# A hybrid decoder layer on one core: compact rotation tables, b and c loaded a block ahead, and the state-space side transfers on another queue

## The chip, the cores and the metric

The kernel runs on 1 core of one Trainium2 chip. The metric is the device time of one execution in microseconds (us), lower is better. The kernel before was run three times: 1270.53, 1271.02 and 1276.63 us, median 1271.02.

## The reference, cut to what matters

One layer of a decoder, computed for a prompt (16 meta tokens and 512 new ones) and for 8 sample tokens; 536 columns in all, of width 2048.

```python
xn = rmsnorm(x, norm_gain)
q, k, v, z_a, u, z_s, g_a, g_s = split(xn @ w_in)          # 2048 x 8704
q, k = rope(rmsnorm(q)), rope(rmsnorm(k))
o_a = sink_attention(q, k, v)         # sliding window of 128, 16 meta keys, a sink
# S5 branch: 64 groups of 16 inputs, 64 complex states each
lam_bar = exp((a_re + i a_im) * dt)
b_bar = (lam_bar - 1) / lam * (b_re + i b_im)
h[t] = lam_bar * h[t-1] + b_bar @ u[t]                     # complex scan over time
y = gelu(real(c @ h) + d_skip * u)
y = y * sigmoid(y @ w_glu + b_glu)
out = x + (sigmoid(g_a) * (o_a * silu(z_a)) @ w_attn_out
         + sigmoid(g_s) * (y * silu(z_s)) @ w_ssm_out) @ w_out
```

The outputs are the new activations, the key and value windows, and the final states.

## The kernel before, in words

The matmuls carry the time. Every weight tile of 128 x 1024 is loaded in float32 (tile `raw`), cast by ScalarE to a reduced-precision high part (`whi`, L1014 or L1080), and VectorE forms the rest (`wlo`, L1015 or L1081). A unit of work, `mm` (L1174), multiplies a weight tile with the activations in 48 matmuls: for each of 8 k-slices high by high, high by low, low by high, two column halves of 260 or 268 each. A large middle part, `quad` (L1410), does the same with four blocks at once, by sums of blocks (L1079) that save products. TensorE runs this stream without a pause if the tiles are there.

Everything else runs as background work. Python generators in three lanes (class `Background`) are stepped between the matmuls: `bg.step` is called after every few k-slices, `yield cost` uses up a budget, and `yield None` ends the lane's turn until the next step. So a `yield None` moves what follows it one step later in TensorE's program. In attention a step is 4 k-slices, 24 matmuls. A scheduler then lays out each engine's queue in an order by its own estimate of times; on the chip each queue runs strictly in that order. Waiting instructions therefore hold up all that is queued behind them on the same engine, and for a DMA that means on the queue of the engine that issues it: SyncE (SP in the profile) for `nc.sync`, GpSimd (POOL) for `nc.gpsimd`.

The background work that the change touches, in order of time:

- `ssm_prep` (to about 400 us) computes the constants of the state-space branch. Its last part writes the rotation tables: for each of 8 blocks `ub`, four products (L308), a difference (L310) and a sum (L311) on VectorE make the table in one scratch tile `t[0]` of 128 x 528, and two DMAs (L314) write it to the DRAM tensor `tabD`, each row of 66 numbers twice, so that the real and the imaginary half of a head lie side by side. The scratch tile is the same for each block, so the products of the next block wait until both DMAs have read it.
- `ssm_consts` (about 450 to 710 us, one pass for each of 8 blocks) loads `f4` (4 DMAs, L347), `bN` (L349) and `c` (L351) into single buffers, scales `bN` and `c` on ScalarE (12 + 32 small instructions, `times`, L362), loads `B` (L381) and `tab` (L383, from `tabD`), forms the products of `B` with `f4` (L391 to L394), and makes the block's short convolution kernel: a matmul (L411), `k0` (L416, L417), a DMA to DRAM (`kD`, L419) and four DMAs back into the matrix `T` (L421). All these DMAs are on SP.
- `ssm_load` fetches the block's inputs `U` with 12 DMAs from POOL (L440 to L444), after `uD` was stored, on POOL too (L1620).
- `ssm_block` does the block: matmuls of `B` with `U` (L473), multiplication by the table (L487, L488), the sums (L493, L494), two scans with a carry (L507, L501 to L505), multiplication back (L513), the states `H` (L518, L519), matmuls of `T` with `U` (L529) and of `CL` with `H` (L532), the gelu (L539 to L546), and six DMAs on SP that store the result to `yD` (L551, L553).
- Attention starts when the last block is done. It loads the tables of the rotary embedding, the keys, values and queries (`sbw`, L703), rotates them, makes the query tiles `QT` (L795) and then takes the score matmuls (L811, L812). Between the first queries and the first scores it lets `NDELAY` = 3 steps pass. Its result is cast to the tile `A` (L1693), which the matmuls with `w_attn_out` read.

The weight loads of the main stream (`raw`, L1013) share SP with all of this.

Of the kernel before, what the change touches and what calls it, by code (L numbers as in the profile page):

```python
# [8 lines left out]
F32 = mybir.dt.float32  # L9
# [3 lines left out]
ALU = mybir.AluOpType  # L13
AX = mybir.AxisListType
P = 128
L = 66
NB = 2
NC = 132
# [3 lines left out]
def bc(ap, axis, n):  # L22

    a = ap.unsqueeze(axis)
    s = list(a.shape)
    s[axis] = n
    return a.to_broadcast(s)
# [122 lines left out]
def ssm_prep(nc, K, tmp, psum, dram, R, ident, a_prm, later, behind, room):  # L150

    v = OnPool(nc, tmp)
# [5 lines left out]
    t = tmp.tile([P, 32], F32, name="th")  # L158
# [11 lines left out]
    x = tmp.tile([P, 32], F32, name="xr")  # L170
# [8 lines left out]
    n = tmp.tile([P, 2, 32], F32, name="sc_n")  # L179
    k = tmp.tile([P, 2, 32], F32, name="sc_k")  # L180
    r = tmp.tile([P, 2, 32], F32, name="sc_r")
    s = tmp.tile([P, 2, 32], F32, name="sc_s")
    q = tmp.tile([P, 2, 32], F32, name="sc_q")
# [28 lines left out]
    g = tmp.tile([P, 2, 32], F32, name="f_g")  # L212
# [19 lines left out]
    r4 = K["r4"]  # L232
# [45 lines left out]
    c = tmp.tile([P, 2, 32], F32, name="zc")  # L278
# [4 lines left out]
    car = K["car"]  # L283
# [13 lines left out]
    FD = dram.tile([8, 32, P], F32, name="FD")  # L297
    nc.sync.dma_start(out=FD.rearrange("(h k) a s -> (k a) h s", h=2), in_=fts)
    R["FD"] = FD
    yield 0.0  # L300
    R["tabD"] = dram.tile([8, P, 16 * L], F32, name="tabD")
    t = [f.rearrange("p (r a i j) -> p r a i j", r=2, a=4, j=6) for f in (room[:, 0:8 * L], room[:, 8 * L:16 * L])]
    for ub in range(8):
        ps = slice(4 * ub, 4 * ub + 4)
        with behind():
            for r in range(2):
                for e in range(2):
                    v_.tensor_tensor(out=t[r][:, e], in0=bc(T11[:, e, ps], 3, 6), in1=bc(T6[:, r, ps], 2, 11), op=ALU.mult)  # L308
            a, b = (f.rearrange("p r a i j -> p r (a i j)") for f in t)
            v_.tensor_tensor(out=a[:, 0], in0=a[:, 0], in1=b[:, 1], op=ALU.subtract)  # L310
            v_.scalar_tensor_tensor(out=a[:, 1], in0=a[:, 1], scalar=-1.0, in1=b[:, 0], op0=ALU.mult, op1=ALU.subtract)  # L311
            d = R["tabD"][ub].rearrange("p (x r l) -> p x r l", r=2, l=L)
            for r in range(2):
                nc.sync.dma_start(out=d[:, :, r], in_=t[0].rearrange("p r a i j -> p (r a) (i j)"))  # L314
        yield 2.4


# [21 lines left out]
def ssm_consts(nc, pool, dram, R, D, ub, a_bT, a_bN, a_cT, e32, d_skip, later, free):  # L339

    v = nc.vector
    ps = slice(4 * ub, 4 * ub + 4)

    f4 = pool.tile([P, 2, 512], F32, name="f4", bufs=1)
    for j in range(4):
        row = R["FD"][3 - j::4, ps, :].rearrange("i a s -> i (a s)").unsqueeze(0).to_broadcast([32, 2, 512])
        nc.sync.dma_start(out=f4[32 * j:32 * j + 32], in_=row)  # L347
    bN = pool.tile([P, 4, 2, 32], F32, name="bN", bufs=1)
    nc.sync.dma_start(out=bN, in_=a_bN[:, ps])  # L349
    c = pool.tile([P, 4, 2, 32], F32, name="c", bufs=1)  # L350
    nc.sync.dma_start(out=c, in_=a_cT[:, ps])  # L351
    yield 0.0
    yield None

    t1 = pool.tile([P, 4, 2, 4, 32], F32, name="ct1", bufs=1)
    t2 = pool.tile([P, 4, 2, 4, 32], F32, name="ct2", bufs=1)
# [7 lines left out]
    for a in range(4):  # L364
        q = slice(4 * ub + a, 4 * ub + a + 1)
# [2 lines left out]
        times(s2[:, a], bN[:, a], R["nFim"][:, q])  # L368
    yield 0.0
    yield None  # L370
    for r, t in ((0, t1), (1, t2)):
        for k in range(4):
            for a in range(4):
                times(t[:, a, :, k], c[:, a], R["lamp"][:, r, k, 4 * ub + a:4 * ub + a + 1])
            if k % 2:
                yield 0.0
                yield None
    while not free():
        yield None
    B = pool.tile([P, 2, 512], F32, name="B")  # L380
    nc.sync.dma_start(out=B, in_=a_bT[ub])  # L381
    tab = pool.tile([P, 2, 4, 2, L], F32, name="tab")
    nc.sync.dma_start(out=tab.rearrange("p i a r l -> p (i a r l)"), in_=R["tabD"][ub])  # L383
    D["tab"] = tab
    CL = pool.tile([P, 4, 2, 5, 32], F32, name="CL")
    nc.scalar.copy(out=CL[:, :, :, 0], in_=c)
# [28 lines left out]
    k0 = pool.tile([P, P], F32, name="k0", bufs=1)  # L415
    nc.scalar.copy(out=k0[:, 32:P], in_=kp[:, 32:P])  # L416
    v.scalar_tensor_tensor(out=k0[:, 0:32], in0=e32, scalar=d_skip[:, ub:ub + 1], in1=kp[:, 0:32], op0=ALU.mult, op1=ALU.add)  # L417
    kD = dram.tile([P, P], F32, name="kD4", bufs=2)
    nc.sync.dma_start(out=kD, in_=k0)  # L419
    for j in range(4):  # L420
        nc.sync.dma_start(out=R["T"][ub % 2][32 * j:32 * j + 32, :, 32 * j:P], in_=kD.rearrange("(a q) x -> q a x", a=4)[:, :, 0:P - 32 * j])  # L421
    yield 0.3

    D["tab"] = tab
    d0 = R["d0"][ub % 2]
    d0v = d0.rearrange("p (a r) l -> p a r l", r=2)
    for i in range(2):
        nc.scalar.copy(out=d0v[:, :, i, 1:L], in_=bc(R["r4"][:, ps], 2, L - 1))
    D["d0"] = d0
    yield 0.0  # L430

# [15 lines left out]
def ssm_block(nc, pool, R, D, ub, y_out, later):  # L447
# [2 lines left out]

    v = nc.vector
    U, T = R["U"][ub % 2], R["T"][ub % 2]
    w = pool.tile([P, NB, 4, 2, L], F32, name="w", bufs=1)

    H = R["H"]
    ps = slice(4 * ub, 4 * ub + 4)
    nc.scalar.copy(out=H[:, :, :, 0:8], in_=R["N0"][:, ps])
    yield None
    tab = D["tab"]
# [17 lines left out]
    p1 = pool.tile([P, 2, 4, NB, L], F32, name="p1", tag="rt1", bufs=1)  # L477
    p2 = pool.tile([P, 2, 4, NB, L], F32, name="p2", tag="rt2", bufs=1)
    for h in range(2):
        for i in range(2):  # L480
            parts = [(slice(0, 2), bu[2 if h else i][:, 0:280].rearrange("p (e c) -> p e c", e=2))]
            if (h, i) == (1, 1):
                parts = [(slice(e, e + 1), place(1, 1, e).unsqueeze(1)) for e in range(2)]
            for es, b in parts:
                a = slice(2 * h + es.start, 2 * h + es.stop)
                bi = b[:, :, 0:NC].rearrange("p e (n l) -> p e n l", l=L)
                v.tensor_tensor(out=p1[:, i, a], in0=bi, in1=bc(tab[:, 0, a, 0], 2, NB), op=ALU.mult)  # L487
                v.tensor_tensor(out=p2[:, i, a], in0=bi, in1=bc(tab[:, 1, a, 0], 2, NB), op=ALU.mult)  # L488
                g = slice(4 * ub + a.start, 4 * ub + a.stop)
                v.tensor_tensor(out=R["sst"][:, g, i], in0=R["A0"][:, g, i], in1=b[:, :, NC:140], op=ALU.add)  # L490
        yield 2.2
    wv = w.rearrange("p n a r l -> p r a n l")
    v.tensor_tensor(out=wv[:, 0], in0=p1[:, 0], in1=p2[:, 1], op=ALU.subtract)  # L493
    v.tensor_tensor(out=wv[:, 1], in0=p1[:, 1], in1=p2[:, 0], op=ALU.add)  # L494
    yield 1.4
    for n in range(NB):
        if n:
            g = w[:, n - 1, :, :, L - 1]
            k1 = pool.tile([P, 4, 2], F32, name="k1", bufs=1)
            k2 = pool.tile([P, 4, 2], F32, name="k2", bufs=1)  # L500
            v.tensor_tensor(out=k1, in0=g, in1=bc(R["car"][:, 0, ps], 2, 2), op=ALU.mult)  # L501
            v.tensor_tensor(out=k2, in0=g, in1=bc(R["car"][:, 1, ps], 2, 2), op=ALU.mult)
            v.tensor_tensor(out=k1[:, :, 0], in0=k1[:, :, 0], in1=k2[:, :, 1], op=ALU.subtract)
            v.tensor_tensor(out=k1[:, :, 1], in0=k1[:, :, 1], in1=k2[:, :, 0], op=ALU.add)
            v.tensor_tensor(out=w[:, n, :, :, 0], in0=w[:, n, :, :, 0], in1=k1, op=ALU.add)  # L505
        wf = w[:, n].rearrange("p a r l -> p (a r l)")
        v.tensor_tensor_scan(out=wf, data0=D["d0"].rearrange("p a l -> p (a l)"), data1=wf, initial=0.0,  # L507
                             op0=ALU.mult, op1=ALU.add)
        yield 1.3 + 0.8 * n
    t1 = pool.tile([P, NB, 4, 2, L], F32, name="rt1", bufs=1)  # L510
    t2 = pool.tile([P, NB, 4, 2, L], F32, name="rt2", bufs=1)
    for t, i in ((t1, 0), (t2, 1)):
        v.tensor_tensor(out=t.rearrange("p n a r l -> p n (a r l)"), in0=w.rearrange("p n a r l -> p n (a r l)"),  # L513
                        in1=bc(tab[:, i].rearrange("p a r l -> p (a r l)"), 1, NB), op=ALU.mult)
    yield 2.5
    hv, v1, v2 = (t.rearrange(f"p {o} -> p r a n l", l=L) for t, o in
                  ((H[:, :, :, 9:9 + NC], "a r (n l)"), (t1, "n a r l"), (t2, "n a r l")))
    v.tensor_tensor(out=hv[:, 0], in0=v1[:, 0], in1=v2[:, 1], op=ALU.add)  # L518
    v.tensor_tensor(out=hv[:, 1], in0=v2[:, 0], in1=v1[:, 1], op=ALU.subtract)  # L519
    yield 1.4  # L520
# [4 lines left out]
    with later():  # L525
        for e in range(2):
            o = [bu[n][:, 140 * e:140 * e + 140] for n in range(2)]
# [8 lines left out]
    ga = pool.tile([P, 4, 140], F32, name="g", bufs=1)  # L536
    o = [(ga[:, n::2], bu[n][:, 0:280].rearrange("p (e c) -> p e c", e=2)) for n in range(2)]
# [9 lines left out]
    dst = y_out.rearrange("(a q) c -> q a c", a=4)  # L547
    for r in range(4):
        s, c = divmod(r, 2)
        o = 260 * c + 128 * s  # L550
        nc.sync.dma_start(out=dst[:, :, o:o + 128], in_=ga[32 * r:32 * r + 32, :, 12:8 + NC])  # L551
    for c in range(2):
        nc.sync.dma_start(out=dst[:, :, 260 * c + 256:260 * c + 260], in_=ga[0:32, :, 4 * c:4 * c + 4])  # L553
    yield 0.8


# [383 lines left out]
BUDGET2, BUDGET3, BUDGET4 = 6.0, 3.4, 4.8  # L940
HIGH = 4000
NLOAD = 3
NDELAY = 3
ATTC = (("kg", 1), ("kgs", 1), ("qg", 1), ("qgs", 1), ("mown", P), ("mprev", P), ("bd64", 4), ("sink", 16))
NXR = 10
NWARM = 9
# [1043 lines left out]
```

## Time and profile before

| | |
|---|---|
| median of 3 runs | 1271.02 us |
| the profiled execution | 1277.01 us, of it a span of 1275.2 us from the first to the last instruction |
| mean granted TensorE clock | 0.992 |
| TensorE matmul busy | 1254.0 us (98%), 10333 instructions |
| VectorE, ScalarE, GpSimd busy | 983.8, 632.1, 267.0 us |
| DMA | 226.75 MB, mean 178 GB/s |

In the profile PE is TensorE, DVE VectorE, ACT ScalarE. A row of a group or of the timeline names the line of the kernel, the engine, the operation, the tile written and the tiles read; brackets give the time that the engine sat idle before it and what ended that. The granted clock is 1.00 at full speed.

### The profile page before, as it was taken

The numbers are of one execution on the slowest core, as the hardware profiler recorded it, in microseconds if no ns is written. First come the engines' busy times: TensorE is split into PE (matmuls) and PEld (weight loads), VectorE is DVE, ScalarE is ACT, GpSimd is POOL, SyncE is SP. The second block draws the span as 40 slices with busy tenths as digits, with TensorE's granted clock in tenths as the row PEclk, the third lists the DMA queues.
The fourth block names the chain that finished last, engine by engine and source line by source line (L and its number), as shares of the span: only waits on it lengthen the run. The fifth ranks groups of instructions, "written<-read, shape, count | busy, mean of one in ns | idle before, by whom it ended". The sixth has DMA issues, their size and how long they took to land.

```text
span 1275.2 us, 26461 instructions
## 1 busy us (share of the span) xinstructions
PE 1254.0 (98%) x10333; PEld 1229.2 (96%) x10333; DVE 983.8 (77%) x1516; ACT 632.1 (50%) x1351; POOL 267.0 (21%) x437
## 2 busy tenths in 40 slices
PE   9999999999899999999999999999999999999998
PEld 9999999999889999999999998999999999999998
DVE  8686888888688755788879666979987467787775
ACT  8554444454344577555552243577665323354442
POOL 0003999930000014123232013120011000000000
PEclk9999999999899999989999998999999999999999
DMA  8544343344887475666665488677667665564441
GB/s 290 204 157 156 123 142 125 125 162 132 167 184 185 144 244 163 166 194 194 174 168 146 139 244 242 197 249 211 193 205 232 225 190 180 160 207 149 153 140 51
DMA packets 125728, 226.75 MB, mean 178 GB/s; under 512 B 38700, under 2 KB 64260, under 8 KB 125572
## 3 DMA queue, kind: packets, MB, share of 16 engines
q1 hardware_dynamic: 116964, 206.63, 53.0%
q0 software_dynamic: 8640, 18.45, 5.7%
q8 instruction: 81, 1.33, 0.4%
q14 instruction: 43, 0.35, 0.1%
HBM read 185.34 MB, written 40.59 MB: 177 GB/s over the span
## 4 chain that ended last, share of the span: by engine, by line
PE 81%; DMA 9%; DVE 5%; issue 2%; SPq 2%; ACT 1%; POOL 0%; DVEq 0%; POOLq 0%; ACTq 0%
PE mm L1174 39%; PE pr L1410 32%; DMA tabD<-work 3%; PE wg L860 2%; DMA sbw<-rawD 1%; PE aux L1410 1%; DMA xr<-in_x 1%; PE aux L1174 1%; DMA raw<-in_w 1%; DMA U<-uD 1%; PE aux L811 1%; PE aux L812 1%; DMA yD<-g 1%; PE mm L1731 1%; PE tr L842 1%
## 5 line engine op out<-in xcount | busy, mean ns | idle before, releaser
L1080 ACT CAST whi<-raw 128x1024 fp32r<-128x1024 f32 x168 | 173.2, 1049 | 186.0 <-DVE raw L1079 95.3
L1081 DVE TENSOR_TENSOR wlo<-raw,whi 128x1024 fp32r<-128x1024 f32 x168 | 206.8, 1252 | 57.8 <-ACT whi L1080 57.5
L1410 PE MATMUL pr<-tau,whi 128*128 128x260 f32 x992 | 182.0, 285 | 6.7 <-DVE z L1445 5.1
L1174 PE MATMUL mm<-xh,whi 128*128 128x260 f32 (+1 forms) x744 | 176.0, 289 | 1.4 <-DVE z L1211 0.8
L1014 ACT CAST whi<-raw 128x1024 fp32r<-128x1024 f32 (+3 forms) x124 | 118.2, 962 | 119.1 <-PE mm L1174 65.1
L1174 PE MATMUL mm<-xl,whi 128*128 128x260 f32 (+1 forms) x744 | 173.4, 286 | 0.0
L1174 PE MATMUL mm<-xh,wlo 128*128 128x260 f32 (+1 forms) x744 | 172.4, 286 | 0.0
L1015 DVE TENSOR_TENSOR wlo<-raw,whi 128x1024 fp32r<-128x1024 f32 (+3 forms) x124 | 137.6, 1118 | 37.2 <-ACT whi L1014 34.8
L1410 PEld LDWEIGHTS pr<-tau,whi 128*128 128x128 f32 x992 | 154.3, 190 | 7.1 <-DVE z L1445 5.3
L1410 PE MATMUL pr<-cb,whi 128*128 128x260 f32 x848 | 153.0, 283 | 0.0
L1410 PE MATMUL pr<-tau,wlo 128*128 128x260 f32 x496 | 140.6, 284 | 0.0
L1410 PEld LDWEIGHTS pr<-cb,whi 128*128 128x128 f32 x848 | 130.8, 189 | 0.2 <-ACT z L1444 0.2
L1174 PEld LDWEIGHTS mm<-xh,whi 128*128 128x128 f32 x744 | 124.7, 189 | 4.0 <-issue 2.2
L1174 PEld LDWEIGHTS mm<-xl,whi 128*128 128x128 f32 x744 | 124.9, 190 | 0.4 <-issue 0.4
L1174 PEld LDWEIGHTS mm<-xh,wlo 128*128 128x128 f32 x744 | 124.1, 189 | 0.0
L1079 DVE TENSOR_TENSOR raw<-raw 128x1024 f32<-128x1024 f32 x95 | 119.0, 1253 | 1.5
L1410 PE MATMUL pr<-cb,wlo 128*128 128x260 f32 x424 | 119.1, 283 | 0.2 <-DVE wlo L1081 0.2
L1410 PE MATMUL pr<-xl,whi 128*128 128x260 f32 x376 | 105.4, 283 | 0.0
L1174 PE MATMUL mm<-Y,whi 128*128 128x260 f32 x576 | 105.3, 286 | 0.0
L1410 PE MATMUL pr<-xh,wlo 128*128 128x260 f32 x376 | 104.9, 283 | 0.0
L1410 PE MATMUL pr<-xh,whi 128*128 128x260 f32 x376 | 104.7, 284 | 0.0
L1410 PEld LDWEIGHTS pr<-tau,wlo 128*128 128x128 f32 x496 | 94.1, 190 | 0.0
(426 smaller groups left out, 2974.0 us busy)
## 6 DMA issues: line engine op xcount, KB each, us to landing
raw<-in_w SPq DMA_DIRECT2D x202, 512.0 KB
gD<-z SPq DMA_DIRECT2D x36, 260.0 KB
t<-gD SPq DMA_DIRECT2D x32, 260.0 KB
cache<-in_vc POOLq DMA_DIRECT2D x16, 286.0 KB, 3.6
cache<-in_kc POOLq DMA_DIRECT2D x15, 288.0 KB, 3.6
xr<-in_x SPq DMA_DIRECT2D x16, 268.0 KB
xg<-in_x SPq DMA_DIRECT2D x8, 536.0 KB
tabD<-work SPq DMA_DIRECT2D x16, 264.0 KB
```

Source lines behind the costliest of these rows:

```text
L811: nc.tensor.matmul(ps[:, e, 0:272], lhsT=q, rhs=KH[:, k0:k0 + 272], start=True, stop=False)
L812: nc.tensor.matmul(ps[:, e, 0:272], lhsT=q, rhs=KL[:, k0:k0 + 272], start=False, stop=True)
L842: nc.tensor.transpose(out=ps[:, 128 * r:128 * r + 128], in_=Pn[:, r], identity=C["idn"])
L860: nc.tensor.matmul(pv[64 * e:64 * e + 64, 0:256], lhsT=V, rhs=pr[:, e::2], start=(i == 0), stop=(i == len(parts) - 1))
L1014: nc.scalar.copy(out=hi, in_=raw)
L1015: self.dve = nc.vector.tensor_tensor(out=lo, in0=raw, in1=hi.bitcast(F32), op=ALU.subtract).ins
L1079: nc.vector.tensor_tensor(out=o, in0=o, in1=i, op=ALU.add)
L1080: nc.scalar.copy(out=hi, in_=t)
L1081: self.dve = nc.vector.tensor_tensor(out=lo, in0=t, in1=hi.bitcast(F32), op=ALU.subtract).ins
L1174: m = nc.tensor.matmul(ps[:, c, 0:W], lhsT=wt[:, k], rhs=xo(kt, c), start=f, stop=l)
L1410: m = nc.tensor.matmul(bank, lhsT=wt[:, p], rhs=x(p, e), start=first and f and p == 0, stop=l and p == 7, skip_group_check=not first and l ...
L1731: nc.tensor.matmul(ps[:, c, 0:260], lhsT=w2[kt // 8][j][:, kt % 8], rhs=xk(xh, kt, c, 8), start=False, stop=(kt, j) == (15, 1))
```

## The change

1. The tables in `tabD` and `tab` lose the doubled rows: half the bytes, one DMA per block instead of two, whole rows of 2112 bytes. For this the order of axes in `w`, `rt1`, `rt2`, `k1`, `k2` and `d0` becomes (half, head, time) in place of (head, half, time). The operations stay the same in number and size.
2. `bN` and `c` get two buffers each and are loaded one block ahead; the wait step at the start of a pass is left only in the first block. `f4` is loaded after the scaling of `bN` instead of first.
3. The loads of `B`, `tab` and `T` and the stores of `kD` and `yD` move from `nc.sync` to `nc.gpsimd`: 13 DMAs a block.
4. `NDELAY` becomes 4.

```diff
@@ ssm_prep
-    R["tabD"] = dram.tile([8, P, 16 * L], F32, name="tabD")
+    R["tabD"] = dram.tile([8, P, 8 * L], F32, name="tabD")
...
-            d = R["tabD"][ub].rearrange("p (x r l) -> p x r l", r=2, l=L)
-            for r in range(2):
-                nc.sync.dma_start(out=d[:, :, r], in_=t[0].rearrange("p r a i j -> p (r a) (i j)"))
+            nc.sync.dma_start(out=R["tabD"][ub], in_=room[:, 0:8 * L])
@@ ssm_consts
-    f4 = pool.tile([P, 2, 512], F32, name="f4", bufs=1)
-    for j in range(4):
-        row = R["FD"][3 - j::4, ps, :].rearrange("i a s -> i (a s)").unsqueeze(0).to_broadcast([32, 2, 512])
-        nc.sync.dma_start(out=f4[32 * j:32 * j + 32], in_=row)
-    bN = pool.tile([P, 4, 2, 32], F32, name="bN", bufs=1)
-    nc.sync.dma_start(out=bN, in_=a_bN[:, ps])
-    c = pool.tile([P, 4, 2, 32], F32, name="c", bufs=1)
-    nc.sync.dma_start(out=c, in_=a_cT[:, ps])
-    yield 0.0
-    yield None
+    def load_bc(n):
+        q = slice(4 * n, 4 * n + 4)
+        t = [pool.tile([P, 4, 2, 32], F32, name=nm) for nm in ("bN", "c")]
+        for d, a in zip(t, (a_bN, a_cT)):
+            nc.sync.dma_start(out=d, in_=a[:, q])
+        R["next"] = t
+
+    if ub == 0:
+        load_bc(0)
+        yield 0.0
+        yield None
+    bN, c = R["next"]
+    if ub < 7:
+        load_bc(ub + 1)
...
     yield 0.0
     yield None
+    f4 = pool.tile([P, 2, 512], F32, name="f4", bufs=1)
+    for j in range(4):
+        row = R["FD"][3 - j::4, ps, :].rearrange("i a s -> i (a s)").unsqueeze(0).to_broadcast([32, 2, 512])
+        nc.sync.dma_start(out=f4[32 * j:32 * j + 32], in_=row)
...
-    nc.sync.dma_start(out=B, in_=a_bT[ub])
-    tab = pool.tile([P, 2, 4, 2, L], F32, name="tab")
-    nc.sync.dma_start(out=tab.rearrange("p i a r l -> p (i a r l)"), in_=R["tabD"][ub])
+    nc.gpsimd.dma_start(out=B, in_=a_bT[ub])
+    tab = pool.tile([P, 2, 4, L], F32, name="tab")
+    nc.gpsimd.dma_start(out=tab.rearrange("p i a l -> p (i a l)"), in_=R["tabD"][ub])
...
-    nc.sync.dma_start(out=kD, in_=k0)
+    nc.gpsimd.dma_start(out=kD, in_=k0)
     for j in range(4):
-        nc.sync.dma_start(out=R["T"][ub % 2][32 * j:32 * j + 32, :, 32 * j:P], in_=kD.rearrange("(a q) x -> q a x", a=4)[:, :, 0:P - 32 * j])
+        nc.gpsimd.dma_start(out=R["T"][ub % 2][32 * j:32 * j + 32, :, 32 * j:P], in_=kD.rearrange("(a q) x -> q a x", a=4)[:, :, 0:P - 32 * j])
@@ ssm_block
-    w = pool.tile([P, NB, 4, 2, L], F32, name="w", bufs=1)
+    w = pool.tile([P, NB, 2, 4, L], F32, name="w", bufs=1)
...
-                v.tensor_tensor(out=p1[:, i, a], in0=bi, in1=bc(tab[:, 0, a, 0], 2, NB), op=ALU.mult)
+                v.tensor_tensor(out=p1[:, i, a], in0=bi, in1=bc(tab[:, 0, a], 2, NB), op=ALU.mult)
...
-        v.tensor_tensor(out=t.rearrange("p n a r l -> p n (a r l)"), in0=w.rearrange("p n a r l -> p n (a r l)"),
-                        in1=bc(tab[:, i].rearrange("p a r l -> p (a r l)"), 1, NB), op=ALU.mult)
+        v.tensor_tensor(out=t.rearrange("p n r a l -> p (n r) (a l)"), in0=w.rearrange("p n r a l -> p (n r) (a l)"),
+                        in1=bc(tab[:, i].rearrange("p a l -> p (a l)"), 1, 2 * NB), op=ALU.mult)
...
-        nc.sync.dma_start(out=dst[:, :, o:o + 128], in_=ga[32 * r:32 * r + 32, :, 12:8 + NC])
+        nc.gpsimd.dma_start(out=dst[:, :, o:o + 128], in_=ga[32 * r:32 * r + 32, :, 12:8 + NC])
     for c in range(2):
-        nc.sync.dma_start(out=dst[:, :, 260 * c + 256:260 * c + 260], in_=ga[0:32, :, 4 * c:4 * c + 4])
+        nc.gpsimd.dma_start(out=dst[:, :, 260 * c + 256:260 * c + 260], in_=ga[0:32, :, 4 * c:4 * c + 4])
...
-NDELAY = 3
+NDELAY = 4
```

More of the change, by code (lines that the diff above doesn't have):

```diff
@@ L425, in ssm_consts @@
     d0 = R["d0"][ub % 2]
-    d0v = d0.rearrange("p (a r) l -> p a r l", r=2)
     for i in range(2):
-        nc.scalar.copy(out=d0v[:, :, i, 1:L], in_=bc(R["r4"][:, ps], 2, L - 1))
+        nc.scalar.copy(out=d0[:, 4 * i:4 * i + 4, 1:L], in_=bc(R["r4"][:, ps], 2, L - 1))
     D["d0"] = d0
@@ L486, in ssm_block @@
                 bi = b[:, :, 0:NC].rearrange("p e (n l) -> p e n l", l=L)
-                v.tensor_tensor(out=p1[:, i, a], in0=bi, in1=bc(tab[:, 0, a, 0], 2, NB), op=ALU.mult)
-                v.tensor_tensor(out=p2[:, i, a], in0=bi, in1=bc(tab[:, 1, a, 0], 2, NB), op=ALU.mult)
+                v.tensor_tensor(out=p1[:, i, a], in0=bi, in1=bc(tab[:, 0, a], 2, NB), op=ALU.mult)
+                v.tensor_tensor(out=p2[:, i, a], in0=bi, in1=bc(tab[:, 1, a], 2, NB), op=ALU.mult)
                 g = slice(4 * ub + a.start, 4 * ub + a.stop)
@@ L491, in ssm_block @@
         yield 2.2
-    wv = w.rearrange("p n a r l -> p r a n l")
+    wv = w.rearrange("p n r a l -> p r a n l")
     v.tensor_tensor(out=wv[:, 0], in0=p1[:, 0], in1=p2[:, 1], op=ALU.subtract)
@@ L498, in ssm_block @@
             g = w[:, n - 1, :, :, L - 1]
[L499 to L504, printed above, removed]
+            k1 = pool.tile([P, 2, 4], F32, name="k1", bufs=1)
+            k2 = pool.tile([P, 2, 4], F32, name="k2", bufs=1)
+            v.tensor_tensor(out=k1, in0=g, in1=bc(R["car"][:, 0, ps], 1, 2), op=ALU.mult)
+            v.tensor_tensor(out=k2, in0=g, in1=bc(R["car"][:, 1, ps], 1, 2), op=ALU.mult)
+            v.tensor_tensor(out=k1[:, 0], in0=k1[:, 0], in1=k2[:, 1], op=ALU.subtract)
+            v.tensor_tensor(out=k1[:, 1], in0=k1[:, 1], in1=k2[:, 0], op=ALU.add)
             v.tensor_tensor(out=w[:, n, :, :, 0], in0=w[:, n, :, :, 0], in1=k1, op=ALU.add)
-        wf = w[:, n].rearrange("p a r l -> p (a r l)")
+        wf = w[:, n].rearrange("p r a l -> p (r a l)")
         v.tensor_tensor_scan(out=wf, data0=D["d0"].rearrange("p a l -> p (a l)"), data1=wf, initial=0.0,
@@ L509, in ssm_block @@
         yield 1.3 + 0.8 * n
-    t1 = pool.tile([P, NB, 4, 2, L], F32, name="rt1", bufs=1)
-    t2 = pool.tile([P, NB, 4, 2, L], F32, name="rt2", bufs=1)
+    t1 = pool.tile([P, NB, 2, 4, L], F32, name="rt1", bufs=1)
+    t2 = pool.tile([P, NB, 2, 4, L], F32, name="rt2", bufs=1)
     for t, i in ((t1, 0), (t2, 1)):
-        v.tensor_tensor(out=t.rearrange("p n a r l -> p n (a r l)"), in0=w.rearrange("p n a r l -> p n (a r l)"),
-                        in1=bc(tab[:, i].rearrange("p a r l -> p (a r l)"), 1, NB), op=ALU.mult)
+        v.tensor_tensor(out=t.rearrange("p n r a l -> p (n r) (a l)"), in0=w.rearrange("p n r a l -> p (n r) (a l)"),
+                        in1=bc(tab[:, i].rearrange("p a l -> p (a l)"), 1, 2 * NB), op=ALU.mult)
     yield 2.5
     hv, v1, v2 = (t.rearrange(f"p {o} -> p r a n l", l=L) for t, o in
-                  ((H[:, :, :, 9:9 + NC], "a r (n l)"), (t1, "n a r l"), (t2, "n a r l")))
+                  ((H[:, :, :, 9:9 + NC], "a r (n l)"), (t1, "n r a l"), (t2, "n r a l")))
     v.tensor_tensor(out=hv[:, 0], in0=v1[:, 0], in1=v2[:, 1], op=ALU.add)
```

## The prediction

> **What bounds the kernel now.** I read the page first, for the engines' shares, then TensorE's waits, then the busy time in windows around each of these waits, then the chain and the timeline backwards from each wait to its cause.
>
> ```profile
> span 1275.2 us, 26461 instructions
> PE 1254.0 (98%) x10333; PEld 1229.2 (96%) x10333; DVE 983.8 (77%) x1516; ACT 632.1 (50%) x1351; POOL 267.0 (21%) x437
> ```
>
> TensorE is busy in all but 21.2 us, and the change takes no matmul away. So it can win only pauses and what a pause does to the clock. TensorE's waits, longest first (total, times, longest):
>
> ```profile
> PE pr L1410 <- DVE z L1445: 5.1, 1, 5.1
> PE aux L811 <- DVE QT L795: 3.1, 2, 2.4
> PE tr L532 <- DVE H L518: 2.9, 1, 2.9
> PE pr L1410 <- DVE t L1445: 1.6, 1, 1.6
> PE aux L473 <- DMA U<-uD: 0.8, 1, 0.8
> ```
>
> Four waits are over 1.5 us. The windows around them (window, its length, busy time and instructions of PE, PEld, DVE, ACT and POOL, then granted clock, DMA share, GB/s), and an undisturbed stretch for comparison:
>
> ```profile
> 337.50:350.00 12.50, 7.42 (x48) 7.22 (x47) 7.72 (x12) 2.10 (x3) 0.00 (x0) 0.73 0.69 112
> 365.00:367.50 2.50, 0.88 (x8) 0.67 (x7) 2.50 (x7) 0.92 (x1) 0.00 (x0) 1.00 0.93 333
> 540.00:550.00 10.00, 7.11 (x43) 6.03 (x42) 8.38 (x11) 5.02 (x14) 5.92 (x11) 0.66 0.78 210
> 775.00:787.50 12.50, 9.36 (x53) 8.84 (x53) 12.14 (x21) 5.90 (x9) 4.64 (x9) 0.73 0.83 258
> 755.00:775.00 20.00, 20.00 (x170) 19.99 (x169) 12.46 (x24) 7.12 (x18) 10.19 (x20) 1.00 1.01 271
> ```
>
> Undisturbed, 170 matmuls take 20 us, 8.5 per us. After the waits of 5.1, 2.9 and 2.4 us the clock is down in the window; after that of 1.6 us it stays at 1.00. The price of a wait is thus more than the wait. First (A): 12.5 x 8.5 = 106 matmuls fit, 48 ran, 58 / 8.5 = **6.8 us** lost. Small one beside it (A2): 2.50 - 0.88 = **1.6**. Second (B): by count (85 - 43) / 8.5 = 4.9, too low since 16 of the 43 are short ones of L411; by idle time (10 - 7.11 = 2.9) and clock (10 x 0.34 = 3.4) 6.3, too high since some of the slow time is idle: I take **5.9**. Third (C): (106 - 53) / 8.5 = **6.2**. Together 20.5 us.
>
> The Trainium skill's "TensorE: Matmul & The Clock Gate" (Part 1, the HAM clock gate) has the clock fall after an idle window of about 3.4 us. By that B and C would keep the clock and cost only their waits, 2.9 and 3.1, and the sum below would end at 1277.0 - 8.4 - 2.9 - 2.2 + 0.6 = 1264.1. The measured clocks of 0.66 and 0.73 decide: it does fall after 2.4 us here, and the matmuls missing in the windows are counted; I give 1264.1 no chance of its own.
>
> **What stands behind each wait.** A: the chain, the products' wait on the scratch tile, and the DMA rows:
>
> ```profile
> 329.70 10.03 DMA tabD<-work
> ...
> 355.96 8.59 DMA tabD<-work
> ```
> ```profile
> DVE work L308 <- DMA tabD<-work: 15.7, 5, 6.6
> ```
> ```profile
> tabD<-work SPq DMA_DIRECT2D x16, 264.0 KB
> uD<-uf POOLq DMA_DIRECT2D x8, 268.0 KB, 2.4
> ```
>
> VectorE stood 6.6 us before the next product because two DMAs of the table were still reading the scratch tile, 10.03 us in the chain; the sums that TensorE needed (L1445) were queued behind it. The second row ends at 364.6, just ahead of A2. B: ScalarE, VectorE and SP rows, in the order of cause:
>
> ```profile
> 526.79 0.85 SPq L351 DMA_DIRECT2D c<-in_cT  x1
> 532.58 5.61 ACT L362 ACTIVATE ct<-c,kept 128x64 f32<-128x64 f32 x23 [8.64 <-DMA c<-in_cT]
> 541.58 1.23 DVE L1015 TENSOR_TENSOR wlo<-raw,whi 128x1024 fp32r<-128x1024 f32 x1 [5.57 <-ACT whi L1014]
> 542.73 0.70 DVE L518 TENSOR_TENSOR H<-rt,rt 128x528 f32<-128x528 f32 x1
> ```
> ```profile
> ACT ct L362 <- DMA c<-in_cT: 24.4, 6, 8.6
> ```
>
> `c` was issued only at 526.79, after its single buffer came free; ScalarE stood 8.64 us, the cast of the next weights lay behind the scalings, VectorE stood 5.57 us for it, and `H` behind that came late. Six of the blocks have such a wait, one reaches TensorE. C: the first scores wait twice, 2.40 + 0.73:
>
> ```profile
> 778.11 0.49 PE L811 MATMUL aux<-KH,QT 128*128 128x272 f32 x1 [2.40 <-DVE QT L795]
> 779.57 0.59 PE L811 MATMUL aux<-KH,QT 128*128 128x272 f32 x1 [0.73 <-DVE QT L795]
> ```
>
> **The change, part by part.** *Tables in one DMA.* Two DMAs of 264 KB become one of 264 KB in rows of 2112 bytes. Its nearest row is the store `uD`, 268 KB of long rows from SBUF to DRAM, 2.4 us to landing. From 10.03 to 2.4, upper bound the 10.03 halved, 5.0. A's wait shrinks by 7.6 to 5.0 us against the 5.1 that TensorE stood: it goes, and A2, of the same chain, with it. Gain 6.8 + 1.6 = 8.4.
>
> *The axes.* Same operations and sizes; if the new patterns cost VectorE something, the 128x1056 products (L513) would rise from 1.22 to that of the sums, 2 x 0.71:
>
> ```profile
> 533.59 2.43 DVE L513 TENSOR_TENSOR rt<-w,tab 128x1056 f32<-128x1056 f32 x2
> ```
>
> That is at most 0.4 us a block, on an engine that is not the bound. Cost taken as 0, between 0 and 0.4 x 8 = 3.2.
>
> *`bN` and `c` a block ahead.* The loads are issued a whole pass earlier, into a second buffer, so the 24.4 us of waits go. B's chain then starts 8.64 us earlier, against the 2.9 that TensorE stood. Next in line is VectorE's own work: L513 (the fence above) ends at 536.0, the rest of the weights takes 1.23, `H` 0.70, so `H` is there at 537.9, and TensorE stood from 543.4 - 2.9 = 540.5. Gain 5.9. `f4` is issued later, but still ahead of the scalings of `c` (23 of them take 5.61), and its reader comes after all 32: no cost. The dropped `yield None` brings each later pass one step forward; that moves nothing that was late.
>
> *Off SP, onto POOL.* These waits leave SP, and the weight loads behind them on that queue are no longer held up:
>
> ```profile
> SPq L383 <- DVE rt L513: 14.7, 4, 4.0
> SPq L421 <- DMA kD<-k: 9.4, 4, 3.4
> SPq L551 <- DVE g L546: 9.2, 5, 4.4
> ```
>
> None of TensorE's five waits names a weight load, so the gain from this alone is 0. The waits themselves move to POOL, where the loads of `U` and the stores `uD` are queued behind them. POOL's price per DMA is this (ns, then landing in us):
>
> ```profile
> L440 POOL DMA_DIRECT2D U<-uD x32: 549/549/585, 480.4 to 692.2; - x32
> DMA to landing us min/median/max: 2.1/3.2/5.2
> ```
>
> 13 DMAs x 0.55 = 7.2 us more per block on POOL, over 8 blocks 57, beside 65.8 of 270 now (the last fence below): it fits. The step with a deadline is `T`. Block 4 as an example:
>
> ```profile
> 613.31 0.23 DVE L417 SCALAR_TENSOR_TENSOR k<-k_e,k_dsk,aux 128x32 f32<-128x32 f32 x1
> 631.36 0.40 PE L529 MATMUL tr<-U,T 128*128 128x140 f32 x2
> ```
>
> From `k0` to its use are 17.8 us. Needed: `kD` 0.55 + 2.4 (as `uD`), four `T` 2.2, landing 3.2 to 5.2, in all 8.4 to 10.4. Left over are 7 to 9 us, which cover any one of the waits above (4.4 at most). The load that has no cover is `U` of the block for which L473 already waits 0.8: with one more issue ahead of it, +0.6 (0 to 4.4).
>
> *`NDELAY` 4.* The scores come one step, 24 matmuls, later: 24 / 8.5 = 2.8 us. They waited 3.13 in all. But attention begins when the last `yD` has landed, and that is now POOL's. Before, on SP (chain), after the last gelu step:
>
> ```profile
> 736.91 3.09 DMA yD<-g
> ```
> ```profile
> 733.63 0.44 DVE L546 SCALAR_TENSOR_TENSOR g<-g,wg 128x280 f32<-128x280 f32 x1
> ```
>
> Landed at 740.0 before. On POOL: 734.1 + 6 x 0.55 + 3.2 = 740.6 (739.5 to 742.6). So the queries come 0.6 later, and 3.13 + 0.6 - 2.8 = 0.9 us of wait remain, too short for the clock (A2). C's gain 6.2 - 0.9 = 5.3. Later scores must not make the end late; the last cast of `A` against its first use:
>
> ```profile
> 1001.62 4.32 ACT L1693 CAST A<-oT 128x520 fp32r<-128x520 f32 x8 [1.12 <-DVE oT L930]
> 1016.86 0.64 PE L1174 MATMUL mm<-A,whi 128*128 128x260 f32 x4
> ```
>
> 1016.86 - 1005.94 = 10.9 us of cover for 2.8 + 0.6.
>
> **The sum.** The profiled execution took 1277.01, 1.8 more than its span. 1277.0 - 8.4 (A, A2) - 5.9 (B) - 5.3 (C) + 0.6 (`U`) = **1258.0**. The median of the three runs is 1271.02, 6 us below the profiled run; the third, 1276.63, is like the profiled one. 6 us is the price of one B or C, so I take it that the two quicker runs lack one of them. What is left when all are gone is the same then, and nothing is subtracted again: the gain is 13 us against the median, 1.0%. If the 6 us are something else, 1252 comes out.
>
> **Rivals.**
>
> *C stays.* If attention starts 1.5 us later than I reckon (the `yD` landings at their longest give 2.0), the wait is 0.9 + 1.5 = 2.4 again and the clock falls: 1258.0 + 5.3 = 1263.3. For it, the 0.73 that a step never covered; against it, the median landing.
>
> *POOL's order makes one or two blocks late.* POOL's queue is in order, and a `T` or `U` behind a stretched wait (4.4, and 3.4 for `kD`, together 7.8) uses up the 7 to 9 us of cover. Each such block costs about a B, 5.9: 1264 or 1270. Against: the two waits would have to fall together.
>
> *POOL's order makes the blocks late throughout.* The same, in six of eight blocks, since each has the same pattern: 1258.0 + 6 x 5.9 = 1293, slower than before. It turns slower from four blocks on. Against: the cover of 7 us and more, and a POOL that is idle most of the stage (the next fence).
>
> *POOL is kept from issuing.* If an issue of POOL had to wait out a VectorE instruction, the 26 DMAs a block (these 13, `uD` and 12 for `U`) would take 26 x (0.55 + 1.23, the length of L1015) = 46 us, over the 34 that a block has (270 / 8): 8 x 12 = 96 us more, 1354. The rows speak against it:
>
> ```profile
> 470.00:740.00 270.00, 265.40 (x2226) 260.80 (x2225) 204.77 (x410) 143.11 (x448) 65.80 (x117) 0.99 0.59 167
> ```
>
> VectorE is busy 204.77 of 270, yet the 32 issues of L440 took 549 to 585 ns. The Trainium skill's "SBUF — State Buffer" (the "DVE blocks DMA" trap) states this lock for copies in VectorE's two-port mode and advises the other queue; the rows of this stage show tensor-tensor products and scans, to which it does not apply.
>
> *The table is not quick.* Under the weight loads one DMA may land in 5 us and more; half of A stays: 1262.
>
> *New pauses in place of the old.* The queues' order comes from estimates; with other DMAs it changes everywhere, and two new waits of B's size give 1270, no change to be told. This is the case in which the change does not do what it says.
>
> **How the numbers follow.** Forecast 0.52; C stays 0.13; one or two blocks 0.10; table 0.05; new pauses 0.12; throughout 0.06; POOL kept 0.02. About 0.5%, 6.4 us, is what a measurement of this kernel can tell from no change, so faster is below 1264.7, slower above 1277.4. Faster: 0.52, and of C stays 0.11, of late blocks 0.06, of the table 0.04, of new pauses 0.02, in all 0.75; slower 0.06 + 0.02 = 0.08; same the rest, 0.17. Range 1251.5 (the 6 us subtracted) to 1268: it takes in the forecast, C, the table and one late block, and leaves out the last cases and part of the new pauses.
>
> **What would show it.** Right: no wait of VectorE for `tabD` over 2 us, and one DMA of about 2.4 us in the chain; no wait of L362 for `c`; clock 1.00 in all windows from 300 to 1000; L811 waiting about 1 us; POOL about 57 us busier. Wrong: a wait of L529 or L473 over 2 us with a low clock behind it; POOL issues well above 585 ns; TensorE's waits as long in total as before at other lines.

## The result, and the profile after

The changed kernel takes 1260.94 us (median of four runs, 1259.92 to 1261.84) against 1271.17 us of the kernel before (four runs, 1270.53 to 1276.63): ratio 0.9910, 95% interval 0.9881 to 0.9938. The forecast was 1258.0. The profiled execution took 1259.92 us, 17.1 less than the profiled one of before. First its page, to be read beside the page of before:

```profile
span 1258.1 us, 26470 instructions
PE 1245.8 (99%) x10333; PEld 1221.6 (97%) x10333; DVE 986.4 (78%) x1516; ACT 632.5 (50%) x1351; POOL 324.4 (26%) x541
```

TensorE stands idle for 12.3 us instead of 21.2, and its busy time is 8.2 us shorter with the same 10333 matmuls: that part is the clock, in the mean 1.000 instead of 0.992. POOL is 57.4 us busier, by the 104 DMAs. TensorE's waits:

```profile
PE mm L1179 <- ACT A L1698: 2.4, 1, 2.4
PE aux L816 <- DVE QT L800: 2.0, 1, 2.0
PE aux L1271 <- ACT whi L1019: 1.2, 2, 1.0
PE tr L1232 <- DVE var L1286: 1.1, 1, 1.1
PE aux L816 <- DVE S L822: 0.7, 2, 0.5
```

The waits for `z` and `t` of L1445, for `H` and for `U` are gone. The scores still wait 2.0 for the queries, and a wait is new: the first matmul that reads `A`, after attention. VectorE's wait on the scratch tile, and the DMA behind it (dropped to one per block, median us to landing last):

```profile
DVE work L308 <- DMA tabD<-work: 0.6, 2, 0.3
```
```profile
tabD<-work SPq DMA_DIRECT2D x8, 264.0 KB, 2.3
```

It was 15.7 in five waits with 6.6 the longest. The windows in which the clock had been at 0.73, 0.66 and 0.73 (columns as in the prediction):

```profile
337.50:350.00 12.50, 12.50 (x102) 11.94 (x101) 11.99 (x18) 7.90 (x11) 0.00 (x0) 1.00 0.53 155
540.00:550.00 10.00, 10.00 (x84) 10.00 (x83) 2.17 (x5) 9.62 (x33) 5.42 (x10) 1.00 0.63 192
775.00:787.50 12.50, 12.50 (x107) 12.50 (x106) 12.38 (x20) 5.09 (x8) 1.66 (x3) 1.00 0.88 280
```

All are full, and the clock is 1.00 in them as in the whole stretch from 300 to 1000 us. The execution splits well at two events that every layout has: the last matmul of the first stretch of `quad` (113 to 444 us here; a second stretch starts at 1092 us), called the last `quad` matmul in what follows, and the first matmul that reads `A`. The rows, of before and then of after:

```profile
451.86 0.28 PE L1410 MATMUL pr<-tau,wlo 128*128 128x260 f32 x1
1016.86 0.64 PE L1174 MATMUL mm<-A,whi 128*128 128x260 f32 x4
```
```profile
443.64 0.28 PE L1415 MATMUL pr<-tau,wlo 128*128 128x260 f32 x1
...
999.55 1.20 PE L1179 MATMUL mm<-A,whi 128*128 128x260 f32 x6 [2.43 <-ACT A L1698]
```

So 8.2 us are won up to the last `quad` matmul (the stage of A and A2), 9.1 between the two events (555.9 us instead of 565.0, the stage of B and C), and nothing after (258.5 instead of 258.3).

### The profile page after: what moved, and what is told of

The parts are those of the page before. It is cut to its first block, busy times and chain, and to the rows that moved or that the text cites. A ratio compares the mean times of both kernels' runs of the same rounds, so it can differ in the third digit from the quotient of the medians.

```text
span 1258.1 us, 26470 instructions
## 1 busy us (share of the span) xinstructions
PE 1245.8 (99%) x10333; PEld 1221.6 (97%) x10333; DVE 986.4 (78%) x1516; ACT 632.5 (50%) x1351; POOL 324.4 (26%) x541
## 4 chain that ended last, share of the span: by engine, by line
PE 89%; issue 4%; DMA 3%; DVE 2%; POOL 1%; ACT 1%; SPq 0%; DVEq 0%; ACTq 0%; POOLq 0%
PE mm L1179 41%; PE pr L1415 37%; PE mm L1271 2%; PE wg L865 1%; PE aux L1415 1%; PE aux L1179 1%; DMA cache<-in_kc 1%; PE aux L1271 1%; DMA KH<-KH 1%; PE wg L537 1%; PE tr L537 1%; PE aux L816 1%; DMA qD<-x 1%; PE tr L478 0%; PE aux L817 0%
## 5 line engine op out<-in xcount | busy, mean ns | idle before, releaser
L1179 PE MATMUL mm<-xh,whi 128*128 128x260 f32 (+1 forms) x744 | 172.8, 286 | 0.2 <-ACT xr L1244 0.2
```

The lines of the kernel that those rows point to most:

```text
L1179: m = nc.tensor.matmul(ps[:, c, 0:W], lhsT=wt[:, k], rhs=xo(kt, c), start=f, stop=l)
```

## The experiments

The theory to be tested was the prediction's: four parts with a gain each. The rival was that the tables carry it all, and that the other three only shift the waits.

**The tables alone.** Part 1 of the diff, nothing else.

```diff
-    R["tabD"] = dram.tile([8, P, 16 * L], F32, name="tabD")
+    R["tabD"] = dram.tile([8, P, 8 * L], F32, name="tabD")
...
+            nc.sync.dma_start(out=R["tabD"][ub], in_=room[:, 0:8 * L])
```

> The kernel before with the compact tables alone. Theory (the prediction's terms): the wait of VectorE for the table DMAs goes from 15.7 us to under 2, both TensorE waits between 337 and 368 us go, the clock stays 1.00 there: about 8.4 us less than before, near 1262.6; the waits at H and at the first scores may stay. Rival (the tables are hidden anyway, the gain comes from the queue): within 2 us of before.

Measured: 1258.56 us (1256.55 to 1259.90), ratio 0.9900, interval 0.9888 to 0.9913. That is the whole gain and no less than with everything. TensorE's waits (some lines left out), then ScalarE's wait for `c`:

```profile
PE aux L808 <- DVE QT L792: 2.1, 2, 1.2
PE tr L1224 <- DVE var L1278: 1.1, 1, 1.1
PE wg L775 <- DVE x L594: 0.9, 1, 0.9
...
PE tr L529 <- DVE H L515: 0.2, 1, 0.2
```
```profile
ACT ct L360 <- DMA c<-in_cT: 10.6, 5, 3.9
```

`c` is still loaded late, but its longest wait fell from 8.6 to 3.9 us, and the states `H` hold TensorE up for 0.2 us instead of 2.9. The reason for B was gone before anything was loaded ahead. What differs is the place of the load on SP. The last read of `c`, which frees its buffer, and SP's issues in the fourth block, before and then with the tables alone (the load of before, at 526.79, stands in the prediction):

```profile
519.34 0.42 ACT L386 COPY CL<-c 128x256 f32<-128x256 f32 x1
524.35 0.43 SPq L1345 DMA_DIRECT2D rawD<-z  x1
524.82 1.86 SPq L1351 DMA_DIRECT2D rawD<-z  x4
```
```profile
505.87 0.41 ACT L384 COPY CL<-c 128x256 f32<-128x256 f32 x1
508.93 0.37 SPq L349 DMA_DIRECT2D c<-in_cT  x1
509.88 0.38 SPq L1342 DMA_DIRECT2D rawD<-z  x1
```

Before, the buffer was free at 519.8 and the load went out 7.0 us later, behind five stores of `rawD`. Here it is free at 506.3, and the load goes out 2.6 us later, ahead of them.

**Tables, and b and c ahead.** Parts 1 and 2; SP and `NDELAY` 3 stay.

```diff
...
+    bN, c = R["next"]
+    if ub < 7:
+        load_bc(ub + 1)
...
```

> Compact tables and b, c a block ahead; queues and NDELAY as before. Theory: no wait of L362 for c (24.4 us before), no TensorE wait at H; 0 to 5.9 us under the tables alone, 5.9 if the quicker runs of before had the wait at H, 0 if they had not. Rival: a wait of the same size at another line of the same stage, and no gain over the tables alone.

Measured: 1260.58 us (1259.96 to 1261.74), 0.9919, interval 0.9906 to 0.9931. The waits for `c` are gone, as they should be, and nothing is won by it. In the profiled run the time is given back at the first scores (waits, then the window around them):

```profile
PE aux L816 <- DVE QT L800: 3.2, 2, 2.5
```
```profile
757.50:770.00 12.50, 9.31 (x53) 8.79 (x52) 12.25 (x20) 5.90 (x9) 4.27 (x8) 0.73 0.75 227
```

It is C, with 53 matmuls in 12.5 us as in the window of before.

**Everything but the queue.** Parts 1, 2 and 4.

```diff
-    nc.gpsimd.dma_start(out=B, in_=a_bT[ub])
+    nc.sync.dma_start(out=B, in_=a_bT[ub])
...
-        nc.gpsimd.dma_start(out=dst[:, :, o:o + 128], in_=ga[32 * r:32 * r + 32, :, 12:8 + NC])
+        nc.sync.dma_start(out=dst[:, :, o:o + 128], in_=ga[32 * r:32 * r + 32, :, 12:8 + NC])
```

> The changed kernel with B, tab, kD, T and yD left on SP. Theory of the prediction: the queue is worth 0 to 0.6 us, so 1260 to 1261. Second theory, from the trace of after: POOL's longer queue makes the planner lay the state-space blocks and so attention some 100 matmuls later in TensorE's program, and the end of attention then holds up the matmuls with A (2.4 us); with the queue undone the first value transposes come back to about 1965 matmuls into that part instead of 2097, no wait for A, about 2.5 us under the changed kernel, near 1258.4.

Measured: 1261.39 us (1260.22 to 1266.24), 0.9931, interval 0.9917 to 0.9945. The wait for `A` is gone, but the time isn't lower: waits of the same size stand at other lines.

```profile
PE aux L816 <- ACT S L820: 2.8, 2, 1.7
PE wg L783 <- DVE x L602: 1.7, 1, 1.7
```

**The queue alone.** Part 3 on the kernel before: its 13 DMAs a block go to `nc.gpsimd`, by the lines of the last diff the other way round.

> The kernel before with the five transfers on POOL alone. Prediction: 0 to 0.6 us over before. Second theory: attention is laid later by some 100 matmuls (12 us), which uses up the 10.9 us of cover of A, so a wait at the first matmuls with A of 1 us or more and 0 to 5 us over before. Rival (the queue carries the gain): 5 us or more under before.

Measured: 1271.06 us (1268.38 to 1274.67), 0.9998, interval 0.9986 to 1.0010. By itself the move is worth nothing in the median. Yet it too removes the wait for `H`: in the fourth block `c` goes out 0.5 us after its buffer came free, and ScalarE's longest wait for it is 4.2 us instead of 8.6. And it changes the program: counted in the traces, 1883 main-stream matmuls (L1174 into `mm`) stand between the last `quad` matmul and the value transposes of attention (L778) in the kernel before, 2024 with this move alone. All runs with the move have 2011 to 2029, all without it 1883. So the order that the scheduler writes puts attention some 140 matmuls later, 140 / 8.5 = 16 us of TensorE's time, before the chip has done anything.

**Tables and `NDELAY` 4.**

```diff
-NDELAY = 3
+NDELAY = 4
```

> Compact tables and NDELAY 4, nothing else: the version that the runs so far point to. The tables alone had 2.1 us of waits left at the first scores (two waits, 1.2 the longest, no fall of the clock) and attention ended far ahead of A. If a step later covers them: about 2 us under the tables alone, near 1256.5. Rival: the step only moves the wait to later scores, and the time stays within 1 us of the tables alone, 1258.6.

Measured: 1260.64 us (1258.98 to 1262.34), 0.9911, interval 0.9892 to 0.9930. The scores' wait for the queries falls to 0.9, and others appear behind it:

```profile
PE aux L808 <- ACT S L812: 2.0, 2, 1.6
PE mm L1171 <- DVE Y L1691: 2.0, 1, 2.0
PE aux L1263 <- ACT whi L1011: 1.3, 2, 1.0
...
PE aux L808 <- DVE S L814: 1.0, 1, 1.0
PE aux L808 <- DVE QT L792: 0.9, 1, 0.9
```

**`NDELAY` 4 alone**, the same edit on the kernel before.

> The kernel before with NDELAY 4 alone. Prediction's term: the wait at the first scores shrinks from 3.1 to about 0.3, 2.8 us less, and 5.3 less where the clock fell there, so 1266 to 1268.7. Rival: the planner lays out other orders and the wait returns at another line: within 1.5 us of before.

Measured: 1273.58 us (1270.18 to 1276.22), 1.0012, interval 0.9999 to 1.0025. The wait for `QT` fell from 3.1 to 0.5, with 2.4 for `S` in its place, and A and B stayed. No gain.

**`c` alone a block ahead**, on the kernel before. With the wide tables there is no room for two buffers of both, so `bN` stays as it was and `k0` shares the place of `bb`.

```diff
+    def load_c(n):
+        R["next"] = pool.tile([P, 4, 2, 32], F32, name="c")
+        nc.sync.dma_start(out=R["next"], in_=a_cT[:, 4 * n:4 * n + 4])
...
-    k0 = pool.tile([P, P], F32, name="k0", bufs=1)
+    k0 = pool.tile([P, P], F32, name="k0", tag="bb", bufs=1)
```

> The kernel before with c alone loaded a block ahead into a second buffer (bN and f4 as before, k0 in the slot of bb to make room, since both loads ahead with the wide tables do not fit). Prediction's term: ACT's waits for c go from 24.4 us to about 0, TensorE's wait at H (2.9 and the clock) with them: up to 5.9 us under before, near 1265.6; the wait from the tables stays. Rival from the run with both ahead, which gained nothing over the tables: the wait at H is one of several that any layout of the queues may bring, and the time is within 2 us of before.

Measured: 1268.07 us (1265.92 to 1272.17), 0.9972, interval 0.9960 to 0.9983. No wait for `c` is left and none for `H`, so B did hang on `c`, as the prediction reads it. Of its 5.9 us only 3.5 arrive: the scores wait longer than before.

```profile
PE pr L1418 <- DVE z L1453: 4.6, 1, 4.6
PE aux L819 <- DVE QT L803: 4.5, 2, 3.9
```

**Long rows, but twice.** The tables-alone kernel writes each table two times, both in rows of 2112 bytes: the bytes of before without its short rows.

```diff
-            nc.sync.dma_start(out=R["tabD"][ub], in_=room[:, 0:8 * L])
+            d = R["tabD"][ub].rearrange("p (r x) -> p r x", r=2)
+            for r in range(2):
+                nc.sync.dma_start(out=d[:, r], in_=room[:, 0:8 * L])
```

> The compact-table kernel, but the table is written to DRAM twice, both times in rows of 2112 bytes: the bytes and the number of writes of before, the long rows of the change. If the short rows of 264 bytes were the price: a pair lands in 3 to 5 us, VectorE's waits for it under 4 us in all, no TensorE wait at 337 to 368 us, time as with the tables alone, 1258.6. If the bytes were the price: VectorE waits 10 us or more, and TensorE stands 3 us or more there.

Measured: 1261.30 us (1258.06 to 1263.39), 0.9916, interval 0.9894 to 0.9939. VectorE's wait and the DMA row:

```profile
DVE work L308 <- DMA tabD<-work: 0.4, 1, 0.4
```
```profile
tabD<-work SPq DMA_DIRECT2D x16, 264.0 KB, 4.8
```

As many stores and stored bytes as before, and the wait of 15.7 us is 0.4. The price of A was the short rows. The last `quad` matmul starts at 443.2 us, as with the tables alone; the 2.7 us over that kernel in the median come later, with waits of 3.2 for `QT` and 2.0 for `H`.

The last three complete the table of what can be put on top of the tables.

**Everything but `NDELAY` 4** (the changed kernel with `NDELAY = 3`).

> The whole change with NDELAY left at 3. If the fourth step of delay is worthless, as the runs with the tables and it suggest, this is 1259 to 1262 us, like the changed kernel's 1260.9, and the 2.4 us wait of the first matmul with the cast of A (attention too late) shrinks, since attention lies one step, 24 matmuls, earlier. The theory of the prediction, that the fourth step buys 5.3 us at the first scores, says 1266, with a wait of the first scores near 3 us and a low clock behind it.

Measured: 1258.80 us (1257.09 to 1260.09), 0.9899, interval 0.9875 to 0.9924. The wait for `A` is gone, and that for the queries is only 0.7 without the fourth step; 2.0 stand at another place, at 847 us:

```profile
PE mm L1179 <- ACT t L1755: 2.0, 1, 2.0
...
PE aux L816 <- DVE QT L800: 0.7, 1, 0.7
```

**Everything but b and c ahead** (the changed kernel with the old start of `ssm_consts`).

> The whole change without b and c ahead. If loading ahead is worth nothing once the tables are quick, this is 1259 to 1262 us, with waits of ScalarE for c of about 4 us and no wait of TensorE for the block's states over 1.5 us. If the loading ahead is what removes the wait for the states in the changed kernel, as the prediction has it, that wait of about 2.9 us is back and the time is about 1266 us.

Measured: 1261.14 us (1260.13 to 1262.40), 0.9915, interval 0.9893 to 0.9936. `c` makes ScalarE wait 3.3 at the longest and no wait for `H` is back. Instead the scores wait 3.4.

**Tables and queue.**

> The tables and the queue move, without the other two. If the queue move is worth nothing by itself in the compact layout too, this is 1258 to 1260 us, like the tables alone (1258.6), and the block's value transposes lie near place 2100 in TensorE's program where the tables alone have them at 1961. If the later place costs cover at the end of attention, the first matmul with the cast of A waits 1 to 2.5 us and the time is 1260 to 1262 us.

Measured: 1262.95 us (1262.58 to 1263.27), 0.9928, interval 0.9909 to 0.9948. Neither case that was written down: the place is that of the move, 2011, as expected, but the loss isn't at `A`, it is at the scores (waits, then SP's waits, then the window):

```profile
PE aux L808 <- DVE QT L792: 7.1, 1, 7.1
```
```profile
SPq L700 <- DMA out_k<-sbw: 8.4, 2, 7.1
```
```profile
765.00:777.50 12.50, 5.36 (x29) 5.16 (x28) 9.21 (x15) 3.32 (x5) 2.00 (x4) 0.64 0.85 231
```

On SP the load of the next query tile (L700) waits 7.1 us for a buffer that the store `out_k` still reads; with b and c ahead (the run of everything but `NDELAY` 4) the longest such wait is 0.8. The pair with `NDELAY` 4 shows the same, 6.8 without b and c ahead and 0.9 with. Each was traced in one profile; that this order alone makes the difference was not tried.

All eight combinations on top of the tables, as ratios to the kernel before on the same chip, and the length of the stretch between the two events in the profiled run of each (us):

| on top of the tables | ratio on SP | stretch | ratio on POOL | stretch |
|---|---|---|---|---|
| nothing | 0.9900 | 552.7 | 0.9928 | 559.2 |
| b, c ahead | 0.9919 | 556.5 | 0.9899 | 553.2 |
| `NDELAY` 4 | 0.9911 | 558.3 | 0.9915 | 558.4 |
| both | 0.9931 | 556.9 | 0.9910 | 555.9 |

The last `quad` matmul starts at 443.2 to 443.9 us in each profile with compact tables, the one with two long rows among them, and at 450.7 to 452.2 in each without. The stretch after the first `A` is 258.3 to 258.8 in all. So everything that the other three parts do is in the middle, within 6.5 us, and no part has a sign of its own there: in the medians b and c ahead cost 0.2% on SP twice and win 0.3% or 0.05% on POOL, and `NDELAY` 4 costs 0.1% in three places of four and wins 0.1% where the queries are latest. The intervals reach 0.12 to 0.28% to either side, and only one pair of the table is apart by them, the tables alone (0.9900) and everything but the queue (0.9931).

## Why the prediction was right in the total and wrong in its steps

**A and A2: right, in mechanism and size.** 8.4 forecast, 8.2 measured at the last `quad` matmul. The prediction named one DMA and long rows together; the run with two long rows shows that the rows are what counts. The DMA that had no row of its own was priced at 2.4 after the nearest row, and lands in 2.3. The axes cost nothing: the products of L513 take 1.253 us instead of 1.256.

**B: right chain, wrong addition.** The wait for `H` did come from `c`; loading `c` ahead alone removes it. But `c` was not held by its single buffer, as the prediction has it: it stood 7.0 us in SP's order after the buffer was free, and the tables alone (0.2 us left) or the move alone, which leave one buffer, remove the wait for `H` as well. And the step priced B on the profile of before and then added it to the tables' gain. With the tables quick, the wait for `H` is 0.2 us, and b and c ahead on SP find nothing left to win (+2.0 us). What the prediction also left out: it is the halved table that makes the room for the second buffers, so this part can't be had whole without the first.

**C: the step that failed.** "C's gain 6.2 - 0.9 = 5.3" did not come. In the changed kernel the scores wait 2.0 for `QT`, not 0.9, and 0.7 for `S`, with the clock at 1.00. Wherever `NDELAY` was raised to 4 without the queue move, `QT` waited less, and `S`, `Y` or `x` stood in its place; alone it gives 1.0012, on the tables 0.9911 against 0.9900. In the changed kernel the fourth step isn't needed for the scores, which wait 0.7 us without it; with it the ratio is 0.9910 against 0.9899, intervals overlapping, so it wins nothing there. It paid once, on POOL without b and c ahead: from 7.1 us of wait to 3.4, where a step is 2.8, and from 1262.95 to 1261.14 us.

**The queue: 0 forecast, 0 measured alone, by other reasons.** The 57 us of POOL and the issue price of 0.55 us were right, and no `T` or `U` came late: no wait of L534, L537 or L478 is left. What the sum left out is that the move changes the program order. The prediction set 10.9 us of cover for `A` against 2.8 + 0.6; in the changed kernel 36 matmuls stand between the last weighing of values (L865, before L860) and the first use of `A` instead of 190, 154 / 8.5 = 18 us less, and the cover is used up. The casts of `A` against the row of the first use shown above:

```profile
998.82 3.27 ACT L1698 CAST A<-oT 128x520 fp32r<-128x520 f32 x6 [8.26 <-DVE oT L935]
```

With the move alone (80 matmuls) `A` is not waited for, and neither is it when one of `NDELAY` (122), b and c ahead (142) or the move (237) is left out of the change: it takes the three together. That this wait is the price of the move, so that leaving SP in place would win it back, fell as well: everything but the queue takes 1261.39 us.

**The rivals.** "New pauses in place of the old" is what came of B, C and the queue, and it was only weighed as a case of its own beside the forecast: the pauses came back in part, within a total that the tables kept low. "C stays" came by half, a wait of 2.0 without a fall of the clock. "The table is not quick" is out, at 2.3 us, and so is "one or two blocks late", with no wait for `T` or `U`. "Late throughout" and "kept from issuing" are out: POOL's issues of `U` take what they took.

```profile
L445 POOL DMA_DIRECT2D U<-uD x32: 549/549/597, 474.0 to 687.2; - x32
```

**The 6 us of the quick runs.** The sum started from a profiled run with a mean clock of 0.992 and took it that the quicker runs lack one fall. Other runs of the kernel before have 0.993 to 0.999, mostly 0.995; at half speed 0.005 x 1270 / 0.5 = 13 us, two falls of 6.8, where 0.992 gives 20, three of them. That supports a missing fall, but not 6 us for it: 6.8 us at half speed lose 3.4 us of TensorE's work, and the rest would have to be a shorter wait. In which place the missing one lies, B or C, was not seen.

**Why the total held.** Median against median 10.2 us were won, 13 forecast. The 8.2 of A stand in the profile, and 6.8 to 9.0 by the range of all profiles with and without compact tables; of the 4.6 that the sum left for B and C after the 6 us, about 2 came, and not by their steps. That the total lies near is in this part luck, and so is it that the new wait for `A` cost 2.4 us and no fall of the clock (the last section). The tables alone give 13.0: the forecast's total, with one of its four parts.

**What stays open.** Which layout of the middle is the best can't be worked out from these runs; single waits of 1 to 3 us come and go with any edit. Why the tables alone put `c` earlier in SP's order was not followed. The best versions are the tables alone and everything but `NDELAY`, ratios 0.9900 and 0.9899; both are about 2 us below the changed kernel in the median, with intervals that overlap its own. The dropped step at the start of a pass and the later `f4` were not tried by themselves.

## What to carry to other kernels

Price each part of a change on the profile that the other parts leave, not on the one of before: a wait that two parts each remove is won once. When a small load comes late, look at what stands ahead of it on its queue before giving it a second buffer. When a DMA is moved to another queue, or a delay is changed, in a kernel whose order a scheduler writes, compare the order first (here the count of matmuls ahead of an event), since it can eat a cover that no duration in the trace would touch. Look at the length of the rows that a store writes before its bytes.

## What the runs showed of the hardware

Two stores of 264 KB in rows of 264 bytes held the source tile for 6.9 to 10.0 us; the same two stores in rows of 2112 bytes cost VectorE a wait of 0.4 us in all. The Trainium skill's "DMA: Bandwidth & Descriptors" (Specifications) says that below 512 bytes the engines read, modify and write; the runs agree with the direction.

A wait's length doesn't settle whether the clock falls; where the wait lies does. In each trace the granted clock is 1.00 or 0.50, and it changes only at the edges of a grid of 3.413 us: in the kernel before at 341.35, 348.18, 542.74, 549.57, 778.26 and 785.08 us, which are 2, 57, 2, 67 and 2 steps of 3.413 apart. Grid windows before (the wait of 2.40 for the scores), after (the wait of 2.43 for `A`) and with everything but b and c ahead (a wait of 1.74):

```profile
774.85:778.26 3.41, 1.01 (x9) 0.80 (x8) 3.35 (x7) 1.51 (x3) 2.01 (x4) 1.00 0.59 187
778.26:781.67 3.41, 2.67 (x11) 2.36 (x12) 3.35 (x6) 2.06 (x4) 2.28 (x5) 0.50 0.72 198
```
```profile
994.63:998.04 3.41, 2.48 (x21) 2.28 (x19) 0.18 (x1) 0.00 (x0) 0.89 (x1) 1.00 0.26 59
998.04:1001.45 3.41, 1.90 (x14) 1.75 (x15) 3.15 (x8) 2.63 (x5) 0.00 (x0) 1.00 0.46 137
1001.46:1004.87 3.41, 3.41 (x31) 3.41 (x30) 3.41 (x5) 2.64 (x5) 0.00 (x0) 1.00 0.72 250
```
```profile
812.50:815.90 3.40, 1.67 (x14) 1.28 (x14) 2.13 (x4) 2.82 (x11) 0.00 (x0) 1.00 1.04 389
815.91:819.32 3.41, 3.41 (x18) 3.41 (x17) 3.21 (x9) 3.36 (x7) 0.54 (x1) 0.50 0.65 224
```

The first wait lies in one window, 2.40 us of it idle, and the clock falls at its end. The grid cuts the wait for `A` into 0.93 and 1.51, and the clock stays. In the 13 traces together, each of the 15 windows at full clock with 2.0 us idle or more is followed by a fall. The least idle time with a fall is 1.73 us (the last pair of rows), the most without one 1.74 (everything but the queue), so the limit is near half a window. A fall lasts one window (3.41 us) where that window has up to 0.37 us of idle time, and two (6.83 us) or three where it has 0.72 and more. The first change to full speed comes at 3.95 to 6.95 us of an execution, so the grid lies differently in each, and the same wait can cost a fall in one and none in the next. The prediction's rival had it that at 2.4 us "the clock falls"; it can, and it need not. The Trainium skill's "TensorE: Matmul & The Clock Gate" (Part 1, the HAM clock gate) has a window of 3413 ns that runs freely; the length of the grid and its place in the traces agree.
